# RG-LRU input product by seven products per pair of tiles, gates of a pair at 1024 columns

## The chip, the cores and the metric

The kernel runs on one core of one Trainium2 chip. The metric is the device time of one execution in microseconds (us); the median over several executions is compared. A profile of one execution gives, for each engine, every instruction with its start and duration.

The engines in this text: PE (TensorE) multiplies matrices into PSUM; ACT (ScalarE) applies functions and copies; DVE (VectorE) does elementwise work, scans and sums; POOL (GpSimd) does elementwise work too; SP issues most of the transfers (DMAs).

## The reference

Two layers on x of 1 x 1024 x 1024 (1024 tokens, 1024 channels), in float32. Layer 0: a retention and gated-delta mixer, then a convolution FFN. Layer 1: an RG-LRU mixer, then a convolution FFN. A norm closes it. The change lies in the mixer of layer 1:

```python
def rglru_mixer(hn, w_in, conv_w, conv_b, w_a, b_a, w_x, b_x, lam, w_out):
    gate, xr = jnp.split(hn @ w_in, 2, axis=-1)
    xr = causal_dwconv(xr, conv_w) + conv_b
    xb = xr.reshape(b, t, LRU_BLOCKS, LRU_BLOCK)
    r = sigmoid(einsum('btni,nij->btnj', xb, w_a) + b_a)
    i = sigmoid(einsum('btni,nij->btnj', xb, w_x) + b_x)
    log_a = -LRU_C * r * softplus(-lam)
    a = jnp.exp(log_a)
    u = jnp.sqrt(-jnp.expm1(2.0 * log_a)) * (i * xr)
    _, hs = lax.associative_scan(_linear_combine, (a, u), axis=1)
    y = gelu(gate) * hs
    return y @ w_out

h = h + rglru_mixer(rms_norm(h, norm_mix), ...)
h = h + conv_ffn(rms_norm(h, norm_ffn), w_up, conv_w, conv_b, w_down)
```

`hn @ w_in` is 1024 x 1024 by 1024 x 2048: 16 output tiles of 128 channels (8 gate tiles, 8 x tiles). The eight blocks of `w_a` and `w_x` are 128 x 128 each, so a tile's gates need that tile alone.

## The kernel before

Channels lie on the 128 partitions, tokens along the row: an activation tile is 128 x 1024, worked on as two halves of 512 columns (`HALF`). The residual is `self.H`, eight such tiles h0 to h7.

**Matmuls.** A float32 product is three matmuls (`mm3`, L313 to L315): weight hi by data hi, weight hi by data lo, weight lo by data hi. A matmul is 128 x 128 weights by 512 columns. Weights arrive from memory in `raw` buffers (seven) and are split by `split_quarter`: hi is a copy on ACT (L267), lo a subtraction on DVE (L268), in a ring of six pairs of buffers (`whi`, `wlo`).

**Pairs in seven products.** The FFN's up product takes two output tiles at once and halves all three dimensions: seven products in place of eight (`pair_products`). Each has 12 matmuls of 512 columns (four 128-row steps by three). The operands are seven combinations of blocks of the normed residual (`operand(o)`) and seven of the weights (`load_pair`; the sums are DVE operations at L288 to L290 and L303). Product o goes to the PSUM bank named by letter o of "ACACABA", so product 2 overwrites the bank of product 0. `pair_sums` empties the banks: products 0 to 2 are copied to `kept` tiles on ACT (L796), products 3 to 5 are added to a kept tile on DVE into the two `halo` tiles (L801), and product 6 is copied by ACT. `pair_halves` does the first pair of a stage on halves of 256 columns, while the second half of the operands is still being built.

**The stage before it.** The down product of layer 0's FFN (`ffn_d0`) runs all eight tiles for columns 0 to 511, then for columns 512 to 1023. Each finished tile half is added to h (L533). `down_x` then scales by the norm's gain and squares, for the norm over channels. Each tile half has 18 matmuls there. `lru_out`, the down product of the RG-LRU mixer, has 24 and ends with `down_pairs`, which also builds the seven operands of the pair scheme on DVE (L616, L626, L631) during its second half, applies the norm (`rtok`, a norm row on PE at L483) and hands over to `pair_halves`.

**RG-LRU mixer (`rglru`).** Sixteen plain products of 48 matmuls. The token norm R is applied when a product leaves PSUM. In step i: `proj_x(i)` (x tile), `stage_x(i)` (convolution: first tap on ACT L1051, three on DVE L1053; then split into hi and lo, L586 and L587), `stage_g(i-1)` (12 gate matmuls; tanh L1070 per half and gate; exp, tanh, sqrt at L1075, L1076, L1082 per half; DVE L1081, L1083, L1084 and scan L1085 per half), `stage_y(i-2)` (gate tile product, gelu L1095, product with the scan's result, stored to `y_dram`). So two products of 48 matmuls lie between the gates of one tile and those of the next. The y tiles come back as operands of `lru_out`.

**Order.** The scheduler orders DVE, ACT, POOL and SP by readiness estimates; every engine executes its queue strictly in order, so a waiting instruction holds up all behind it. PE's order is written by hand in the pair stages (`manual_schedule`).

## Time and profile before

| what | us |
|---|---|
| median of 3 executions | 2153.62 (2153.57 to 2155.07) |
| the profiled execution, its own time | 2152.99 |
| its span, first to last instruction | 2151.2 |
| PE, DVE, ACT, POOL busy | 2137.9, 1693.5, 1082.8, 98.2 |
| second half of `ffn_d0`, from | 1184 |
| RG-LRU products and gates | 1222 to 1416 |
| second half of `lru_out`, to | 1455 to 1497 |

Starts are counted from the first instruction. A busy time adds up the durations of an engine's instructions; a duration includes fill and drain, so back-to-back instructions overlap a little in the record and the start-to-start distance is what a queue full of them costs. The granted clock is 1.00 over the whole execution.

### The profile page before, as it was taken

Reading aid. Unit: us, or ns where it says so; the run is one execution under the profiler, and the core shown is the slowest. Engines: PE = TensorE matmul, PEld = TensorE weight load, DVE = VectorE, ACT = ScalarE, POOL = GpSimd, SP = SyncE. Lnnn points to the kernel's source line nnn. Section 1 sums busy time; section 2 is a strip of 40 time slices with the busy share of each in tenths; the row PEclk is TensorE's granted clock in tenths of the full one; section 3 lists DMA queues with packets and bytes.
Section 4 is the critical chain, followed back from the end, with each engine's and each line's share of the span. In section 5 each row is a group of like instructions: output and inputs, shape, how many; then the busy total and the mean of one; then the engine's idle time right before and its main releaser. Section 6 shows DMA issues by size and latency. Waiting matters only on the chain.

```text
span 2151.2 us, 29709 instructions
## 1 busy us (share of the span) xinstructions
PE 2137.9 (99%) x10716; PEld 1783.3 (83%) x10716; DVE 1693.5 (79%) x2565; ACT 1082.8 (50%) x1748; POOL 98.2 (5%) x114
## 2 busy tenths in 40 slices
PE   9999999999999999999999999999999999999998
PEld 7877889888888888888888888888888888888887
DVE  7995676656999889888866787778999889888645
ACT  6444433235665555555324476756655555554321
POOL 0102022300000000000000000000000000000001
PEclk9999999999999999999999999999999999999999
DMA  5354423444145445437636312242354345375542
GB/s 187 92 168 127 134 89 96 166 128 131 55 155 174 146 158 191 156 109 273 230 104 205 87 54 80 70 154 68 119 180 167 143 159 178 118 266 178 181 169 84
DMA packets 205171, 307.98 MB, mean 143 GB/s; under 512 B 29376, under 2 KB 92384, under 8 KB 205024
## 3 DMA queue, kind: packets, MB, share of 16 engines
q1 hardware_dynamic: 197760, 299.60, 41.9%
q10 hardware_dynamic: 6240, 5.97, 0.9%
q8 instruction: 84, 1.38, 0.3%
q0 software_dynamic: 1024, 0.53, 0.1%
q14 instruction: 63, 0.52, 0.1%
HBM read 215.27 MB, written 90.74 MB: 142 GB/s over the span
## 4 chain that ended last, share of the span: by engine, by line
PE 93%; DVE 3%; DMA 1%; issue 1%; SPq 0%; ACT 0%; POOL 0%; POOLq 0%; DVEq 0%; ACTq 0%
PE ps L313 28%; PE ps L314 28%; PE ps L315 28%; PE pc L313 1%; PE pc L314 1%; PE pc L315 1%; DVE l L1333 0%; DVE l L1331 0%; PE pc L483 0%; DMA l<-gc_dram 0%; DVE wlo L268 0%; PE ps L1508 0%; PE pc L1464 0%; PE ps L1606 0%; PE pc L1576 0%
## 5 line engine op out<-in xcount | busy, mean ns | idle before, releaser
L313 PE MATMUL ps<-s,whi 128*128 128x512 f32 (+1 forms) x2704 | 1054.5, 391 | 1.1 <-ACT s L383 0.7
L314 PE MATMUL ps<-s,whi 128*128 128x512 f32 (+1 forms) x2704 | 1047.9, 388 | 0.5 <-DVE s L900 0.5
L315 PE MATMUL ps<-s,wlo 128*128 128x512 f32 (+1 forms) x2704 | 1047.3, 388 | 0.0
L267 ACT CAST whi<-raw 128x512 fp32r<-128x512 f32 (+1 forms) x620 | 376.6, 613 | 628.4 <-PE ps L314 494.6
L313 PEld LDWEIGHTS ps<-s,whi 128*128 128x128 f32 x2704 | 507.8, 188 | 106.6 <-ACT s L383 1.3
L315 PEld LDWEIGHTS ps<-s,wlo 128*128 128x128 f32 x2704 | 507.7, 188 | 104.7 <-DVE wlo L268 0.6
L314 PEld LDWEIGHTS ps<-s,whi 128*128 128x128 f32 x2704 | 508.1, 188 | 102.5 <-DVE s L900 1.9
L268 DVE TENSOR_TENSOR wlo<-raw,whi 128x512 fp32r<-128x512 f32 (+1 forms) x620 | 415.7, 676 | 72.0 <-ACT whi L267 60.8
L828 DVE SCALAR_TENSOR_TENSOR t<-halo,cols,t 128x1024 f32<-128x1024 f32 x176 | 221.6, 1281 | 2.6 <-ACT t L826 1.6
L801 DVE TENSOR_TENSOR halo<-ps,kept 128x512 f32<-128x512 f32 (+1 forms) x138 | 91.8, 666 | 74.4 <-PE ps L315 73.2
L811 DVE TENSOR_TENSOR h<-ps,h 128x512 f32<-128x512 f32 x112 | 77.3, 690 | 78.8 <-PE ps L315 78.8
L826 ACT ACTIVATE t<-halo,cols 128x1024 f32<-128x1024 f32 x88 | 109.5, 1246 | 18.6 <-DVE halo L801 10.2
L796 ACT COPY kept<-ps 128x512 f32<-128x512 f32 (+1 forms) x138 | 77.1, 558 | 11.0 <-PE ps L315 9.5
L533 DVE TENSOR_TENSOR h<-ps,h 128x512 f32<-128x512 f32 (+1 forms) x72 | 45.2, 630 | 42.4 <-PE ps L315 42.3
L916 DVE TENSOR_TENSOR t<-t 128x1024 f32<-128x1024 f32 x44 | 53.6, 1219 | 0.0
L911 ACT ACTIVATE t<-t 128x1024 f32<-128x1024 f32 x44 | 46.7, 1062 | 10.5 <-DVE t L828 10.5
L852 ACT CAST t<-t 128x512 fp32r<-128x512 f32 x56 | 34.0, 621 | 35.3 <-DVE t L916 33.2
L401 ACT ACTIVATE t<-h 128x512 f32<-128x512 f32 (+1 forms) x49 | 27.3, 562 | 43.6 <-DVE h L533 43.6
L313 PE MATMUL ps<-s,s 128*128 128x256 f32 (+1 forms) x144 | 46.0, 320 | 0.0
L314 PE MATMUL ps<-s,s 128*128 128x256 f32 (+1 forms) x144 | 45.8, 318 | 0.0
L315 PE MATMUL ps<-s,s 128*128 128x256 f32 (+1 forms) x144 | 45.8, 318 | 0.0
L857 DVE TENSOR_TENSOR t<-t 128x512 f32<-128x512 f32 x64 | 43.9, 685 | 0.7 <-DMA sf_dram<-t 0.6
(339 smaller groups left out, 2124.5 us busy)
## 6 DMA issues: line engine op xcount, KB each, us to landing
raw<-in_ffn_up_dram SPq DMA_DIRECT2D x176, 256.0 KB, 2.7
s<-pf_dram SPq DMA_DIRECT2D x112, 256.0 KB, 5.3
sf_dram<-t SPq DMA_DIRECT2D x72, 256.0 KB, 2.5
raw<-in_ffn_w_dram SPq DMA_DIRECT2D x64, 256.0 KB, 2.9
t<-sf_dram SPq DMA_DIRECT2D x58, 256.0 KB, 4.5
pf_dram<-t SPq DMA_DIRECT2D x56, 256.0 KB, 2.6
pf_dram<-lo SPq DMA_DIRECT2D x56, 256.0 KB, 2.5
raw<-in_mix_in_dram SPq DMA_DIRECT2D x52, 256.0 KB, 2.9
```

Of the source, the lines that this page charges most:

```text
L267: self.nc.scalar.copy(hi[:, 0:w], raw[:, 0:w])
L268: eng.tensor_tensor(lo[:, 0:w], raw[:, 0:w], f32(hi[:, 0:w]), ALU.subtract)
L313: mm(ps, whi, xhi, start=start, stop=False)
L314: mm(ps, whi, xlo, start=False, stop=False)
L315: mm(ps, wlo, xhi, start=False, stop=stop)
L796: A.copy(kept[o], ps)
L801: V.tensor_tensor(dst(i, j), v(ps), v(kept[k]), ALU.add)
L811: V.tensor_tensor(h(*to[o]), ps.rearrange("p (h c) -> p h c", c=256), h(*to[o]), ALU.add)
L826: A.activation(t, buf[:, 2:2 + T], AF.Identity, scale=w(0), bias=self.col(f"ffn_cb{layer}", tile_i))
L828: V.scalar_tensor_tensor(t, buf[:, 2 + j:2 + j + T], w(j), t, ALU.mult, ALU.add)
L911: A.activation(tg, tg, AF.Silu)
L916: V.tensor_tensor(tg, tg, tv, ALU.mult)
```

## The change

The 16 input products become eight pairs in seven products (`lru_p`: an x pair, then the gate pair of the same two tiles, four times). The end of `ffn_d0` therefore builds the seven operands, as `lru_out`'s end does, and `down_x` goes. Each half of h is stored to `h_dram` on the way, since the residual's tiles h0 to h7 now serve as buffers of the mixer; they are loaded again ahead of `lru_out`. The gates of the even tile of a pair come after product 5 of the gate pair, those of the odd tile after product 6 (`then`); the rest of the gate work (`stage_h`) is done for both tiles together and 1024 columns at a time, after the last gate. To POOL go the weights' lo parts from the second gate pair to the last (`lo_engine`), the first convolution tap of the odd tiles, and the last product of `stage_y` for three of the four pairs. The small columns (`few`) with the softplus of `lru_lam` move to the kernel's start.

By instruction counts over the kernel: matmuls of 512 columns 8472 before and 8292 now, of 256 columns 624 and 792; POOL elementwise operations of 512 columns 28 and 69, of 1024 columns none and 10, of 256 columns none and 5.

```diff
             if layer == 1:
-                for i in range(8):
-                    o.append((("lru_in", 8 + i), 2))
-                    if i >= 1:
-                        o.append((("lru_g", i - 1), 1))
-                    if i >= 2:
-                        o.append((("lru_in", i - 2), 2))
-                o += [(("lru_g", 7), 1), (("lru_in", 6), 2), (("lru_in", 7), 2)]
+                for t in range(4):
+                    o.append((("lru_p", 2 * t), 7))
+                    o += [(("lru_p", 2 * t + 1), range(6)), (("lru_g", 2 * t), 1)]
+                    o += [(("lru_p", 2 * t + 1), range(6, 7)), (("lru_g", 2 * t + 1), 1)]
                 o += out("lru_out", 0) + out("lru_out", 1)
...
+    def rows(self, key):
+
+        src = self.I["lru_in" if key[0] == "lru_p" else key[0]]
+        if key[0].startswith("ffn_up"):
+            return src[key[1]], src[NPAIR + key[1]]
+        if key[0].startswith("ffn_w"):
+            c, t = key[1:]
+            return src[c, 2 * t], src[c, 2 * t + 1]
+        t, gate = divmod(key[1], 2)
+        first = 2 * t + (0 if gate else 8)
+        return src[first], src[first + 1]
...
-        s = lambda raw: self.split_quarter(raw, V, place=self.extra.pop(len(self.loaded), None))
+        s = lambda raw: self.split_quarter(raw, self.lo_engine, place=self.extra.pop(len(self.loaded), None))
...
-    def down_x(self, ys, name, gain):
+    def down_pairs(self, ys, name, gain, groups=None, keep=None):
 
         def then(n, st, m, h):
-            st["whole"] = True
-            self.square_step(st, m, self.norm_step(st, m, gain, n))
-            if m == KT - 1:
-                if n == 0:
-                    self.norm_beside(st, n)
-                else:
-                    self.steps(8, self.norm_rest(st, n, 3))
-        self.down_norm(ys, name, gain, lambda n: self.groups(1), then)
-
-    def down_pairs(self, ys, name, gain):
-
-        def then(n, st, m, h):
+            if keep is not None:
+                self.nc.sync.dma_start(keep[m][:, n * HALF:(n + 1) * HALF], h)
             st["bufs"] = [self.halo[n][:, 4 + HALF:]] + [b[:, 4:4 + HALF] for b in self.halo]
             st["whole"] = n == 0
             self.square_step(st, m, h)
...
                 if m == 5:
                     self.late = self.late_operands(st, gain)
                 self.late["scale"](m)
-        self.down_norm(ys, name, gain, self.groups, then)
+        self.down_norm(ys, name, gain, groups or self.groups, then)
...
-    def pair_products(self, layer, p, then=None):
-
-        key = (f"ffn_up{layer}", p)
+    def pair_products(self, key, then=None):
...
-            self.down_x(last, f"ffn_d{layer}", gain)
+            self.h_dram = self.tc.dram_tile([KT, P, T], F32, name="h_dram")
+            self.down_pairs(last, f"ffn_d{layer}", gain, lambda n: self.groups(1), self.h_dram)
...
+            if i % 2:
+                nc.gpsimd.tensor_scalar(x, buf[:, 1:1 + T], w(0), self.col("lru_cb", i), ALU.mult, ALU.add)
+            else:
+                A.activation(x, buf[:, 1:1 + T], AF.Identity, scale=w(0), bias=self.col("lru_cb", i))
             for j in (1, 2, 3):
                 V.scalar_tensor_tensor(x, buf[:, 1 + j:1 + j + T], w(j), x, ALU.mult, ALU.add)
-            xh, xl = (xs[:, (2 * (i % 2) + j) * T:(2 * (i % 2) + j + 1) * T] for j in range(2))
+            xh, xl = (self.h_tile(2 * (i % 2) + j, F32R) for j in range(2))
...
-                    A.activation(t, ps, AF.Tanh, scale=0.5, bias=b[:, i:i + 1])
-                    th[n, q] = t
-            for n in range(2):
-                a = u()
-                A.activation(a, th[n, 0], AF.Exp, scale=spm4[:, i:i + 1], bias=spm4[:, i:i + 1])
-                A.activation(th[n, 0], th[n, 0], AF.Tanh, scale=sp2[:, i:i + 1], bias=sp2[:, i:i + 1])
-                th[n, 2] = a
-            for n in range(2):
-                sl = slice(n * HALF, (n + 1) * HALF)
-                sq, tx, a = th[n, 0], th[n, 1], th[n, 2]
-                V.scalar_tensor_tensor(tx, tx, 1.0, x[:, sl], ALU.add, ALU.mult)
-                A.activation(sq, sq, AF.Sqrt)
+                    A.activation(H[2 * (i % 2) + q][:, sl], ps, AF.Tanh, scale=0.5, bias=b[:, i:i + 1])
+        def stage_h(t):
+            decay = [self.h_tile(m) for m in range(2)]
+            two = [(i, H[2 * (i % 2)], H[2 * (i % 2) + 1], decay[i % 2], xr[i][0]) for i in (2 * t, 2 * t + 1)]
+            for i, th, tx, a, x in two:
+                A.activation(a, th, AF.Exp, scale=spm4[:, i:i + 1], bias=spm4[:, i:i + 1])
+                A.activation(th, th, AF.Tanh, scale=sp2[:, i:i + 1], bias=sp2[:, i:i + 1])
+                V.scalar_tensor_tensor(tx, tx, 1.0, x, ALU.add, ALU.mult)
+            for i, sq, tx, a, x in two:
+                A.activation(sq, sq, AF.Sqrt, scale=0.25)
                 V.scalar_tensor_tensor(sq, a, 1.0, sq, ALU.add, ALU.mult)
-                V.scalar_tensor_tensor(tx, tx, 0.5, sq, ALU.mult, ALU.mult)
-                V.tensor_tensor_scan(hs[:, sl], a, tx, 0.0 if n == 0 else hs[:, HALF - 1:HALF], ALU.mult, ALU.add)
-            st[i] = hs
-        def stage_y(i):
-            hs = st.pop(i)
-            unit = self.unit("lru_in", i)
-            def evac(n, sl, ps):
-                g = u() if i < 6 else self.halo[i % 2][:, 4 + sl.start:4 + sl.stop]
-                V.tensor_tensor(g, ps, self.R[:, sl], ALU.mult)
-                A.activation(g, g, AF.Gelu_apprx_tanh)
-                V.tensor_tensor(hs[:, sl], g, hs[:, sl], ALU.mult)
-            self.project(unit, evac)
-            if i < 6:
-                nc.sync.dma_start(self.y_dram[i], hs)
-            return hs
-        proj_x(0)
-        for step in range(8):
-            if step == 0:
-                proj_x(1)
-            elif step > 1:
-                proj_x(step)
-            stage_x(step)
-            if step >= 1:
-                stage_g(step - 1)
-            if step >= 2:
-                stage_y(step - 2)
-        stage_g(7)
-        stack.close()
-        self.open_s2(self.ctx)
-        ys = [self.load_split(self.y_dram[i], self.place2(i)) for i in range(4)]
-        hs = [stage_y(6), stage_y(7)]
-        ys += [self.load_split(self.y_dram[4 + i], self.place1(i)) for i in range(2)]
-        ys += [self.split(hs[i], self.place1(2 + i)) for i in range(2)]
-        self.down_pairs(ys, "lru_out", gain)
+                V.tensor_tensor(tx, tx, sq, ALU.mult)
+                V.tensor_tensor_scan(x, a, tx, 0.0, ALU.mult, ALU.add)
+        def stage_y(t):
+            for i in (2 * t, 2 * t + 1):
+                g = gs[i] = self.R if i % 2 == 0 else f32(self.parts.tile([P, T], F32R, tag="lo", name="lo"))
+                A.activation(g, self.halo[i % 2][:, 4:4 + T], AF.Gelu_apprx_tanh)
+            stage_h(t)
+            for i in (2 * t, 2 * t + 1):
+                (V if t == 3 else nc.gpsimd).tensor_tensor(gs[i], gs[i], xr.pop(i)[0], ALU.mult)
+                if i < 6:
+                    nc.sync.dma_start(self.y_dram[i], gs[i])
+        ys = {}
+        def load_y(*ks):
+            for k in ks:
+                ys[k] = self.load_split(self.y_dram[k], self.place2(k))
+        def then(t, o):
+            if o >= 5:
+                stage_g(2 * t + o - 5)
+            if t == 3 and o in (1, 2, 4):
+                load_y(*{1: (0, 1), 2: (2, 3), 4: (4, 5)}[o])
+        pair = lambda s: ("lru_p", s)
+        with self.tc.manual_schedule(engines={mybir.EngineType.PE}):
+            second = self.pair_products(pair(1), partial(then, 0))
+            self.pair_halves(pair(0), pair(1), second)
+            self.lo_engine = nc.gpsimd
+            stage_x(0)
+            stage_x(1)
+            self.run(second)
+        for t in range(4):
+            if t:
+                self.run(self.pair_products(pair(2 * t)))
+                stage_x(2 * t)
+                stage_x(2 * t + 1)
+                if t == 3:
+                    self.lo_engine = V
+                self.run(self.pair_products(pair(2 * t + 1), partial(then, t)))
+            stage_y(t)
+        H = self.H = [self.h_tile(m) for m in range(KT)]
+        for m in range(4):
+            nc.sync.dma_start(H[m], self.h_dram[m])
+        for i in (6, 7):
+            ys[i] = self.split(gs[i], self.place1(i - 6))
+        self.after(26, lambda: [nc.sync.dma_start(H[m], self.h_dram[m]) for m in range(4, KT)])
+        self.down_pairs([ys[i] for i in range(KT)], "lru_out", gain)
```

**ACT between two steps.** Of before, the row of ACT around one tile's gates (names: `us` small gate tiles, `whi` weight parts, `pc` the PSUM tile of the gate matmuls):

```order
L1070 ACTIVATE us<-pc,ba 128x512
L1051 ACTIVATE t<-halo_99,cols 128x1024
L1070 ACTIVATE us<-pc,bx 128x512
L1070 ACTIVATE us<-pc,ba 128x512
L1070 ACTIVATE us<-pc,bx 128x512
L1075 ACT_TABLE_LOAD
L1075 ACTIVATE us<-us,spm_10748 128x512 x2
L1076 ACTIVATE us<-us,sp_10746 128x512
L586 CAST xs<-t 128x1024
L1076 ACTIVATE us<-us,sp_10746 128x512
L1082 ACT_TABLE_LOAD
L1082 ACTIVATE us<-us 128x512 x2
```

Of the change, ACT from the second tile's last tanh to the first copies of the next pair (`h_...` are the reused residual tiles, `R` and `lo` the gelu tiles, `kept<-ps` the copy that empties product 0's bank):

```order
L1047 ACTIVATE h_10743<-pc,few 128x512
L1065 ACTIVATE lo<-halo_99 128x1024
L1053 ACT_TABLE_LOAD
L1053 ACTIVATE h_11639<-h_10740,few 128x1024
L1053 ACTIVATE h_11640<-h_10742,few 128x1024
L1054 ACTIVATE h_10740<-h_10740,few 128x1024
L1054 ACTIVATE h_10742<-h_10742,few 128x1024
L1057 ACT_TABLE_LOAD
L1057 ACTIVATE h_10740<-h_10740 128x1024
L1057 ACTIVATE h_10742<-h_10742 128x1024
L269 CAST whi<-raw 128x512
L786 COPY kept<-ps 128x512
```

The chain of one tile has become a chain of two tiles at twice the width, and the copy of product 0 of the next pair stands behind all of it. The product that overwrites that bank, product 2, waits on PE for this copy.

**DVE at the same place**, of the change, from the gate chain to the sums of the next pair (`L1058` to `L1060` need the sqrt above; `raw<-raw` are weight sums; `halo<-ps,kept` the sums of products 3 to 5):

```order
L293 TENSOR_TENSOR raw<-raw 128x512
L1055 SCALAR_TENSOR_TENSOR h_10743<-h_10743,t 128x1024
L1058 SCALAR_TENSOR_TENSOR h_10740<-h_11639,h_10740 128x1024
L1058 SCALAR_TENSOR_TENSOR h_10742<-h_11640,h_10742 128x1024
L1059 TENSOR_TENSOR h_10741<-h_10741,h_10740 128x1024
L1059 TENSOR_TENSOR h_10743<-h_10743,h_10742 128x1024
L1060 SCALAR_TENSOR_TENSOR t<-h_11639,h_10741 128x1024
L1060 SCALAR_TENSOR_TENSOR t<-h_11640,h_10743 128x1024
L292 TENSOR_TENSOR raw<-raw 128x512
L306 TENSOR_TENSOR raw<-raw 128x512
L791 TENSOR_TENSOR halo_98<-ps,kept 128x2x256
L791 TENSOR_TENSOR halo_99<-ps,kept 128x2x256
```

The weight sum at `L306` needs a `raw` buffer that a weight lo on POOL reads. The sums of the next pair's products stand behind the scans. On POOL the rows at this place are:

```order
L270 TENSOR_TENSOR wlo<-raw,whi 128x256
L270 TENSOR_TENSOR wlo<-raw,whi 128x512
L270 TENSOR_TENSOR wlo<-raw,whi 128x256
L270 TENSOR_TENSOR wlo<-raw,whi 128x512 x8
L1068 TENSOR_TENSOR R<-R,t 128x1024
L270 TENSOR_TENSOR wlo<-raw,whi 128x512
L1068 TENSOR_TENSOR lo<-lo,t 128x1024
```

**DVE near the end of `ffn_d0`.** Of before, from one addition to h (L533) to the next but one (`s_96` takes the scaled tiles, `t<-t` sums squares):

```order
L533 TENSOR_TENSOR h_89<-ps,h_89 128x512
L268 TENSOR_TENSOR wlo<-raw,whi 128x256
L384 SCALAR_TENSOR_TENSOR s_96<-h_89,cols,s_96 128x512
L405 TENSOR_TENSOR t<-t 128x512
L268 TENSOR_TENSOR wlo<-raw,whi 128x512
L533 TENSOR_TENSOR h_90<-ps,h_90 128x512
L268 TENSOR_TENSOR wlo<-raw,whi 128x256
L384 SCALAR_TENSOR_TENSOR s_96<-h_90,cols,s_96 128x512
L405 TENSOR_TENSOR t<-t 128x512
L268 TENSOR_TENSOR wlo<-raw,whi 128x512
L533 TENSOR_TENSOR h_91<-ps,h_91 128x512
```

Of the change, at the same place, from one addition to h (L536) to the next (`t<-t,pc` scales by the norm, `s_4166<-t,s_4166` and the `t<-t` of 1024 columns build operands):

```order
L536 TENSOR_TENSOR h_89<-ps,h_89 128x512
L624 TENSOR_TENSOR t<-t 128x1024
L408 TENSOR_TENSOR halo_99<-halo_99 128x512
L270 TENSOR_TENSOR wlo<-raw,whi 128x256
L619 TENSOR_TENSOR t<-t,pc 128x1024
L609 TENSOR_TENSOR s_4166<-t,s_4166 128x1024
L270 TENSOR_TENSOR wlo<-raw,whi 128x512
L624 TENSOR_TENSOR t<-t 128x1024
L536 TENSOR_TENSOR h_90<-ps,h_90 128x512
```

Between two additions there were four operations of at most 512 columns; here there are seven, four of them 1024 columns wide.

More of the change, by code (lines that the diff above doesn't have):

```diff
@@ L129, in __init__ @@
         pad(self.perm, 49, "pad1")
-        self.H = [self.perm.tile([P, T], F32, name=f"h{m}") for m in range(KT)]
+        self.H = [self.h_tile(m) for m in range(KT)]
         self.s1 = self.perm.tile([P, 2, 32, 256], F32R, name="s1")
@@ L211, in quarter_order @@
                 o += [x for _ in range(2) for x in out("ffn_d0", 1)]
-        return [(key, j) for key, n in o for j in range(n)]
+        return [(key, j) for key, n in o for j in (range(n) if isinstance(n, int) else n)]
     @staticmethod
@@ L233, in unit @@
         return [self.quarter(key, j, hold) for j in range(2)]
[L235 to L251 removed]
+    def rows(self, key):
[8 more added lines that the diff above has]
+        return src[first], src[first + 1]
+    def load_all(self):
+        pair = None
+        for key, j in self.order[len(self.loaded):]:
+            if key[0].startswith(("ffn_up", "ffn_w", "lru_p")):
+                if j == 0:
+                    pair = self.pairs.pop(key, None) or self.load_pair(key)
+                yield next(pair)
+                continue
+            src = self.I[key[0]]
             for i in key[1:]:
                 src = src[i]
[L254 to L259 removed]
+            c, w = j * HALF, min(HALF, src.shape[1])
+            w = min(w, src.shape[1] - c)
+            raw = self.raw()
+            self.nc.sync.dma_start(raw[:, 0:w], src[:, c:c + w])
+            yield self.split_quarter(raw, self.lo_engine, w)
     def raw(self):
@@ L722, in pair_halves @@
         self.prefetch(first)
-        up = self.I[key[0]]
         self.eager = True
-        pair = self.pairs[key[0], p + 1] = self.load_pair(up[p + 1], up[NPAIR + p + 1])
+        pair = self.pairs[after] = self.load_pair(after)
         next(pair)
@@ L932, in ffn @@
         with self.tc.manual_schedule(engines={mybir.EngineType.PE}):
-            second = self.pair_products(layer, 1, partial(after, 1))
-            self.pair_halves(layer, 0, second)
+            up = lambda p: (f"ffn_up{layer}", p)
+            second = self.pair_products(up(1), partial(after, 1))
+            self.pair_halves(up(0), up(1), second)
             after(0, 5)
@@ L939, in ffn @@
         for p in range(2, NPAIR):
-            self.run(self.pair_products(layer, p, partial(after, p)))
+            self.run(self.pair_products(up(p), partial(after, p)))
             if p < NPAIR - 1:
@@ L1024, in rglru, with sm @@
+        used = [0]
+        def sm(name):
+            used[0] += 8
+            return self.few[:, used[0] - 8:used[0]]
+        sp, sp2, spm4, nl, ba, bx = (sm(n) for n in ("sp", "sp2", "spm4", "nl", "ba", "bx"))
         V.tensor_scalar(nl, self.cols_of("lru_lam"), -1.0, None, ALU.mult)
         self.softplus(sp, nl, sm, "l")
-        sp2 = sm("sp2")
         V.tensor_scalar(sp2, sp, 2.0, None, ALU.mult)
-        spm4 = sm("spm4")
         V.tensor_scalar(spm4, sp, -4.0, None, ALU.mult)
-        ba, bx = sm("ba"), sm("bx")
@@ L1058, in stage_g @@
         def stage_g(i):
-            x, xh, xl = xr.pop(i)
-            hi, lo = self.quarter(("lru_g", i))
-            hs = self.t()
-            th = {}
+            x, xh, xl = xr[i]
+            hi, lo = self.quarter(("lru_g", i), 0, self.hold)
             for n in range(2):
```

60 lines of the change are left out of this document (11 added, 49 removed).

## Prediction

> **What bounds the kernel now.** I read the page first: busy shares, granted clock, chain of waits.
>
> ```profile
> PE 2137.9 (99%) x10716; PEld 1783.3 (83%) x10716; DVE 1693.5 (79%) x2565; ACT 1082.8 (50%) x1748; POOL 98.2 (5%) x114
> PEclk9999999999999999999999999999999999999999
> PE 93%; DVE 3%; DMA 1%; issue 1%; SPq 0%; ACT 0%; POOL 0%; POOLq 0%; DVEq 0%; ACTq 0%
> ```
>
> PE is the bound from end to end, at full clock. Fewer matmuls are worth their whole time, as long as nobody makes PE wait. Then the stages that the change touches, in windows (columns: length; busy us of PE, PEld, DVE, ACT, POOL; clock; DMA share; GB/s):
>
> ```profile
> 1184.00:1217.00 33.00, 33.00 (x154) 26.92 (x152) 24.52 (x50) 19.03 (x32) 2.00 (x5) 1.00 0.40 115
> 1222.00:1392.00 170.00, 170.00 (x752) 140.75 (x751) 125.76 (x163) 116.17 (x158) 0.00 (x0) 1.00 0.21 66
> 1455.00:1497.00 42.00, 42.00 (x197) 34.85 (x190) 38.87 (x52) 27.01 (x49) 1.01 (x1) 1.00 0.24 73
> ```
>
> In the RG-LRU stage (1222 to 1392) PE never waits, with DVE at 74% and ACT at 68% beside it. In the second half of ffn_d0 (1184 on) DVE fills 24.5 of 33 us. In that of lru_out, which also builds pair operands, it fills 38.9 of 42: nearly all. What PE pays per matmul is the distance between starts, in PE's timeline:
>
> ```profile
> 1299.82 0.39 PE L314 MATMUL ps<-s,whi 128*128 128x512 f32 x1
> ...
> 1300.73 0.39 PE L315 MATMUL ps<-s,wlo 128*128 128x512 f32 x1
> ...
> 1503.05 0.28 PE L313 MATMUL ps<-s,whi 128*128 128x256 f32 x1
> ...
> 1503.89 0.28 PE L314 MATMUL ps<-s,whi 128*128 128x256 f32 x1
> ```
>
> Four steps of 512 columns take 0.91, so 0.2267 each; seven of 256 take 0.84, so 0.12 each.
>
> **The gain.** The counts give 180 matmuls of 512 columns fewer and 168 of 256 more: 180 x 0.2267 = 40.8, less 168 x 0.12 = 20.2, is 20.6. The norm sums and row in the middle of the halves cost about 1.1 (one such row below). Net gain 19.5 us. Everything else in the sum is a new wait of PE.
>
> **A, the end of ffn_d0.** DVE now does lru_out's work there, but a tile half has 18 matmuls in place of 24. The additions to h, first and last of the second half, in DVE's timeline, and PE's norm row after lru_out:
>
> ```profile
> 1183.27 0.68 DVE L533 TENSOR_TENSOR h<-ps,h 128x512 f32<-128x512 f32 x1
> ...
> 1211.24 0.69 DVE L533 TENSOR_TENSOR h<-ps,h 128x512 f32<-128x512 f32 x1 [0.68 <-PE ps L315]
> ...
> 1497.15 0.69 DVE L533 TENSOR_TENSOR h<-ps,h 128x512 f32<-128x512 f32 x1
> ...
> 1499.61 0.17 DVE L465 TENSOR_SCALAR rtok<-halo 128x4 f32<-128x4 f32 x1
> 1500.98 1.16 PE L483 MATMUL pc<-ident,rtok 128*128 128x128 f32 x8 [0.25 <-POOL rtok L466]
> ```
>
> The window is 1211.24 - 1183.27 = 28.0 us. Between the same two additions the changed DVE row holds 15 operations of 1024 columns, 24 of 512 and 5 of 256 (order of instructions). Durations and overlap come from these groups and this place of DVE's timeline:
>
> ```profile
> L268 DVE TENSOR_TENSOR wlo<-raw,whi 128x512 fp32r<-128x512 f32 x64 | 42.7, 685 | 15.7 <-ACT whi L267 15.6
> L1053 DVE SCALAR_TENSOR_TENSOR t<-halo,cols,t 128x1024 f32<-128x1024 f32 x24 | 30.8, 1281 | 9.6 <-ACT t L1051 9.5
> L1085 DVE TENSOR_TENSOR_SCAN t<-us 128x512 f32<-128x512 f32 x8 | 9.8, 1219 | 0.0
> L587 DVE TENSOR_TENSOR xs<-t,xs 128x1024 fp32r<-128x1024 f32 x8 | 9.7, 1219 | 0.5 <-ACT xs L586 0.5
> L268 DVE TENSOR_TENSOR wlo<-raw,whi 128x256 fp32r<-128x256 f32 x7 | 2.9, 417 | 0.0
> ...
> 263.58 0.68 DVE L1461 TENSOR_TENSOR kept<-pc,l 128x512 f32<-128x512 f32 x1
> 264.19 0.67 DVE L1465 TENSOR_TENSOR kept<-kept,pc 128x512 f32<-128x512 f32 x1
> ```
>
> A queue's distance is about 0.07 less than the duration: 0.61 for 512 columns, 1.14 for 1024, 0.35 for 256. 15 x 1.14 + 24 x 0.61 + 5 x 0.35 = 33.5, against 28.0: the last addition comes 5.5 late. Behind it seven more of 512 columns stand ahead of rtok: 0.69 + 7 x 0.61 + 0.3 = 5.2, against 1499.61 - 1497.15 = 2.46 in lru_out. PE there waited 0.25 at the norm row with all else equal. A = 5.5 + 2.7 + 0.25 = 8.5. Ends: 5 (the seven are done while PE and ACT make the sums), 11 (the first half leaves DVE a backlog of 2.5).
>
> **B, the first x pair.** Its gates need tile 0's convolution and split, and the halves have drawn part of the gate pair's products ahead, so PE has little between. DVE owes both tiles' six taps, 6 x 1.21 = 7.3, and the even tile's split 1.14. I take 4.5; ends 1 (the taps run in between sums) and 6. The odd tile's tap on POOL has no row for its form; the nearest lie between one of POOL's 512-column operations below (1.28) and two (2.56), and it runs beside the even tile's taps.
>
> **C, the three boundaries between steps.** After the last gate matmul PE has products 0 and 1 of the next x pair, 24 x 0.2267 = 5.44 us (17 matmuls, 3.85, at the first boundary). Product 2 overwrites product 0's bank and so waits for ACT's copy, which ACT's row puts behind the whole gate chain. The chain at 512 columns, in ACT's timeline, and groups that give its length at 1024:
>
> ```profile
> 1389.09 0.67 ACT L1070 ACTIVATE us<-pc,bx 128x512 f32<-128x512 f32 x1
> 1389.78 1.28 ACT L1075 ACT_TABLE_LOAD   x1
> 1391.08 1.52 ACT L1075 ACTIVATE us<-us,spm 128x512 f32<-128x512 f32 x2
> 1392.51 1.51 ACT L1076 ACTIVATE us<-us,sp 128x512 f32<-128x512 f32 x2
> 1394.03 1.28 ACT L1082 ACT_TABLE_LOAD   x1
> 1395.33 1.15 ACT L1082 ACTIVATE us<-us 128x512 f32<-128x512 f32 x2
> 1396.50 1.28 ACT L1095 ACT_TABLE_LOAD   x1
> ...
> L1051 ACT ACTIVATE t<-halo,cols 128x1024 f32<-128x1024 f32 x8 | 9.9, 1235 | 0.6 <-DVE halo L373 0.6
> L1075 ACT ACTIVATE us<-us,spm 128x512 f32<-128x512 f32 x16 | 12.2, 812 | 0.1
> L267 ACT CAST whi<-raw 128x512 fp32r<-128x512 f32 x49 | 29.3, 616 | 37.8 <-PE ps L314 33.9 <-ACT t L608 2.3 <-DMA raw<-in_lru_outa_dram 1.6
> L796 ACT COPY kept<-ps 128x512 f32<-128x512 f32 (+1 forms) x138 | 77.1, 558 | 11.0 <-PE ps L315 9.5
> ```
>
> Six activations with two table loads take 1396.50 - 1389.78 = 6.72 us. Twice the width adds 1235 - 812 = 423 ns each: 6.72 + 6 x 0.42 = 9.3. From the last gate matmul: 0.2 to start, last tanh 0.69, one gelu of 1024 about 1.0, chain 9.3, a weight hi 0.5, the copy 0.56: 12.2. PE waits 12.2 - 5.44 = 6.8, twice, and 12.2 - 3.85 = 8.4 once: C1 = 22. Ends 19 and 24 (one weight hi more or less, a gelu already done).
>
> Behind it comes DVE. Its two STTs, two products, two scans of 1024 columns (about 2.25 each, twice L1085) and two weight sums, 2.4 + 2.3 + 4.5 + 1.2 = 10.4, start at about 11.3 and end at 21.7. The sum of product 4, which product 6 needs, follows; PE by then has ended product 5 at about 22.9. Undisturbed, DVE is just in time. But POOL now works at the same place, and the two engines hold each other up in this trace (DVE's and POOL's timelines, one behind the other):
>
> ```profile
> 261.83 1.28 POOL L1541 TENSOR_TENSOR t<-t,l 128x512 f32<-128x512 f32 x1 [38.55 <-DMA g_dram<-t]
> 263.19 1.62 POOL L1580 TENSOR_TENSOR l<-t,l 128x512 f32<-128x512 f32 x1
> 277.57 1.29 POOL L1541 TENSOR_TENSOR t<-t,l 128x512 f32<-128x512 f32 x1 [6.71 <-DVE l L1540]
> ...
> 262.75 0.92 DVE L268 TENSOR_TENSOR wlo<-raw,whi 128x512 fp32r<-128x512 f32 x1 [1.05 <-PE pc L1460]
> 278.07 1.33 DVE L1452 TENSOR_TENSOR kept<-kept,l 128x512 f32<-128x512 f32 x1
> ```
>
> The DVE subtraction from 262.75 lasts 0.92 in place of 0.685 and ends 0.56 after POOL's end at 263.11; the product from 278.07 lasts 1.33 and ends 0.54 after POOL's at 278.86. Both look as if they stood still until POOL was through. With four POOL weights (1.15 left of each) and one product of 1024 (2.3) taking turns with DVE's chain, DVE ends at 21.7 + 6.9 = 28.6, and PE waits up to 5.7 more at each boundary. Ends of C2: 0 and 18; I take 4 each, 12, nearer the upper end since both rows show the full stand.
>
> [...]
>
> **D, the tail.** After the last gates nothing is left but lru_out, which has 61 matmuls, 13.8 us, before it needs y tile 6. From the last gate matmul: 0.2, tanh 0.69, a table load 1.28, two gelus 2.0, chain 9.3: 13.5. The first sqrt ends 0.6 before that, and DVE runs STTs, products, scans and the last multiplication from 12.9: 2.4 + 2.3 + 4.5 + 1.1 = 10.3, so R's y tile is there at 23.2; cast and split 0.6 each and queue distances bring 24.5 to 25.3. D = 11 (10 to 13).
>
> **Sum.** 2152.99 - 19.5 + 8.5 + 4.5 + 22 + 12 + 11 = 2191.5. The profiled run lies 0.6 below the median of the three, so nothing is added. Costed at nothing: the 16 stores and 8 loads of h and the 6 y tiles, 256 KB halves on SP's queue, which the windows show loaded at 0.21 to 0.40; and the softplus at the start, a few operations of 8 columns (each under 0.2 like L465 above). If SP's queue were late with weights instead, PE would show waits for DMA, some us per pair.
>
> **Rivals.**
> - *POOL and DVE do not get in each other's way here*: C2 is 0 and B about 2. For: DVE has a quarter of idle time in the stage of before. Against: the two rows. 2191.5 - 12 - 2.5 = 2177.
> - *The clock falls in the waits.* The warm-up at the start, PE's timeline:
>
> ```profile
> 1.16 4.15 PE L1624 MATMUL pc<-t 128*128 128x128 f32 x20 [1.16 <-POOL l L1627]
> ```
>
>   20 matmuls of 128 columns in 4.15 us, 0.21 each, where eight of the same size took 1.16 at the norm row, 0.145 each with fill: PE out of idleness ran at about half of what it does later. If each of the six waits of over 4 us brought back one such stretch, at 2 us lost each, 12 us come on top: 2203. Against: before has no wait of that length, so nothing shows it. [...]
> - *The other side: PE does not wait for ACT's copy.* If ACT reaches product 0's copy within the 5.44 us of products 0 and 1, C and most of D go: A 5, B 1, D 11 - 6.8 = 4 remain, 10 in all, against 19.5 gained: 2143.5. The point is 5.4 us from the last gate matmul to the copy, against 12.2 worked out; half of that chain would have to be done before the last gate, and it needs the last tanh. Together the waits must stay under 19.5 us for this kernel to be faster.
>
> **How the numbers follow.** The sum as worked out (within 10 us of 2191.5) 0.45; no contention, 2177, 0.22; clock, 2203 (with upper ends up to 2220), 0.23; the other side, 2143.5, 0.07; about equal 0.03. The lower ends of all terms, 5 + 1 + 19 + 0 + 10 = 35 less 19.5, give 2168.5; a boundary wait half as long as I make it gives 2160. The upper ends, 11 + 6 + 24 + 18 + 13 = 72, give 2205.5, and with the clock 2218. So 2160 to 2218. A measurement of this kernel can tell about 0.2%, 4.3 us, from no change: faster 0.07, same 0.03, slower 0.90.
>
> **What would show it.** In the changed profile: PE idle of 5 to 11 us at the end of ffn_d0, released by POOL's or DVE's rtok; three idle stretches of 6 to 9 us released by the ACT copy of product 0 (or by the weight hi ahead of it), each 17 to 24 matmuls behind the last gate; a second, shorter one in the same pair released by a DVE sum; one of about 11 us ahead of lru_out's second half, released by DVE. The DVE operations of 1024 columns beside POOL work would last longer than 1.28, and POOL's weight lo longer than 1.28. The clock row would show less than 9 in slices 22 to 28 if the second rival holds. I am wrong if PE is as full as before in these stages, or if its waits have DMA as the releaser.

## The result, and the profile after

The change takes 2229.88 us (median of four executions, 2226.89 to 2231.84) against 2153.6: a ratio of 1.0352, 95% interval 1.0334 to 1.037. The sign of the forecast was right, its size was not: 2191.5 was forecast, and 2218 was the end of its range. The profiled execution took 2231.84, its span is 2230.1 (before 2152.99 and 2151.2). The kernel before, timed again beside each group of experiments below, had medians of 2153.47 to 2154.2, so their times can be compared. One execution of the last kernel below (the tail in order) took 4339.42 us and is left out of its median.

The page of the change, busy shares and the clock row:

```profile
PE 2149.0 (96%) x10728; PEld 1786.8 (80%) x10728; DVE 1736.7 (78%) x2536; ACT 1105.7 (50%) x1793; POOL 198.1 (9%) x166
PEclk9999999999999999999999988889999999999999
```

PE is no longer full, and four slices of the clock row, those of the mixer, show an 8; the mean granted clock is 0.981, against 0.999 before, where it falls only in the last 6.4 us (0.50 there). What PE waited for between 1180 and 1520 us, in the view of waits (columns: us in total, times, longest):

```profile
PE ps L316 <- ACT whi L269: 26.3, 4, 9.1
PE ps L316 <- DVE halo L791: 17.0, 4, 5.6
PE ps L316 <- ACT s L579: 6.4, 1, 6.4
PE pc L316 <- ACT h L579: 3.1, 1, 3.1
PE pc L477 <- ACT halo L404: 2.9, 1, 2.9
PE pc L477 <- DVE halo L408: 2.4, 1, 2.4
PE ps L316 <- ACT kept L786: 1.9, 2, 1.0
PE pc L486 <- POOL rtok L469: 1.8, 1, 1.8
```

First row: the three waits at product 2 (9.1 the longest) and one of 2.9 at the tail. Second: the three waits for the sum of product 4, and one of 1.6 ahead of lru_out. Third: the y tile at the tail. Fourth: the first x pair. The rows for L477 and L486 are the norm at the end of ffn_d0, and `kept` is two short waits for copies. The chain ahead of product 2, in ACT's timeline:

```profile
1286.88 1.28 ACT L1053 ACT_TABLE_LOAD   x1
1288.18 2.37 ACT L1053 ACTIVATE h<-h,few 128x1024 f32<-128x1024 f32 x2
1290.45 2.36 ACT L1054 ACTIVATE h<-h,few 128x1024 f32<-128x1024 f32 x2
1292.83 1.28 ACT L1057 ACT_TABLE_LOAD   x1
1294.13 2.00 ACT L1057 ACTIVATE h<-h 128x1024 f32<-128x1024 f32 x2
1296.04 0.60 ACT L269 CAST whi<-raw 128x512 fp32r<-128x512 f32 x1
1296.55 0.58 ACT L786 COPY kept<-ps 128x512 f32<-128x512 f32 x1
```

ACT never pauses. From the first table load to the end of the sqrts it takes 9.2 us (9.3 forecast); weight hi and copy stand behind, the copy from 1296.55, though product 0's last matmul started at 1284.48. Then PE and its clock, in PE's timeline of the same place:

```profile
1287.21 0.39 PE L318 MATMUL ps<-s,wlo 128*128 128x512 f32 x1
1296.69 1.28 PE L316 MATMUL ps<-s,whi 128*128 128x512 f32 x2 [9.10 <-ACT whi L269]
1297.77 0.63 PE L317 MATMUL ps<-s,whi 128*128 128x512 f32 x1
1298.19 0.63 PE L318 MATMUL ps<-s,wlo 128*128 128x512 f32 x1
...
1302.72 0.40 PE L317 MATMUL ps<-s,whi 128*128 128x512 f32 x1
1302.95 0.39 PE L318 MATMUL ps<-s,wlo 128*128 128x512 f32 x1
```

Behind the wait, matmuls start 0.43 us apart in place of 0.23, for some 5 us; the granted clock from 1280 to 1303 us is 0.78. So the second rival held as well as the forecast.

A ledger follows from the distances between starts of PE's matmuls: what exceeds 0.2267 or 0.12 is a wait where the distance is more than 2.4 times that, else slow clock. Stages are cut at the additions to h. A wait by these distances is some 0.15 us longer than in the view of waits.

| part | forecast | in the profiled execution |
|---|---|---|
| fewer matmuls, net | -19.5 | -18.5 |
| A, end of ffn_d0 | 8.5 | 7.6 |
| B, first x pair | 4.5 | 3.2 |
| C1, product 2 | 22 | 23.8 |
| C2, product 6 | 12 | 15.9 |
| D, tail | 11 | 10.8 |
| waits under 2 us elsewhere | 0 | 8.9 |
| low clock behind waits | 0 (12 in the rival) | 19.5 |
| start of the kernel | 0 | 7.8 |
| sum | 38.5 | 79 |

The last row is the difference of the spans, 78.9.

### The profile page after: what moved, and what is told of

Its sections match the earlier page's. It is cut to its first block, busy times and chain, and to the rows that moved or that the text cites. A ratio compares the mean times of both kernels' runs of the same rounds, so it can differ in the third digit from the quotient of the medians.

```text
span 2230.1 us, 29926 instructions
## 1 busy us (share of the span) xinstructions
PE 2149.0 (96%) x10728; PEld 1786.8 (80%) x10728; DVE 1736.7 (78%) x2536; ACT 1105.7 (50%) x1793; POOL 198.1 (9%) x166
## 3 DMA queue, kind: packets, MB, share of 16 engines
q0 software_dynamic: 1024, 0.53, 0.1%
## 5 line engine op out<-in xcount | busy, mean ns | idle before, releaser
L269 ACT CAST whi<-raw 128x512 fp32r<-128x512 f32 (+1 forms) x643 | 390.4, 613 | 651.1 <-PE ps L317 483.1
L270 DVE TENSOR_TENSOR wlo<-raw,whi 128x512 fp32r<-128x512 f32 (+1 forms) x597 | 401.2, 678 | 65.9 <-ACT whi L269 54.9
L818 DVE SCALAR_TENSOR_TENSOR t<-halo,cols,t 128x1024 f32<-128x1024 f32 x176 | 221.5, 1280 | 2.1 <-ACT t L816 1.0
L791 DVE TENSOR_TENSOR halo<-ps,kept 128x512 f32<-128x512 f32 (+1 forms) x165 | 108.2, 658 | 79.4 <-PE ps L318 78.4
L786 ACT COPY kept<-ps 128x512 f32<-128x512 f32 (+1 forms) x165 | 91.4, 554 | 16.3 <-PE ps L318 14.1
L469 POOL TENSOR_TENSOR rtok<-rtok,npow 128x4 f32<-128x4 f32 (+1 forms) x10 | 9.9, 993 | 960.6 <-PE ps L316 608.6
L270 POOL TENSOR_TENSOR wlo<-raw,whi 128x512 fp32r<-128x512 f32 (+1 forms) x46 | 74.0, 1622 | 80.3 <-ACT whi L269 77.2
L536 DVE TENSOR_TENSOR h<-ps,h 128x512 f32<-128x512 f32 (+1 forms) x72 | 45.1, 629 | 38.7 <-PE ps L318 38.6
L306 DVE TENSOR_TENSOR raw<-raw 128x512 f32<-128x512 f32 x68 | 53.1, 781 | 8.0 <-POOL wlo L270 7.4
L605 ACT CAST s<-t 128x1024 fp32r<-128x1024 f32 x39 | 40.9, 1050 | 34.3 <-DVE t L677 18.8
L291 DVE TENSOR_TENSOR raw<-raw 128x512 f32<-128x512 f32 x68 | 46.9, 689 | 13.1 <-POOL wlo L270 11.2
L292 DVE TENSOR_TENSOR raw<-raw 128x512 f32<-128x512 f32 x68 | 53.0, 780 | 0.5
```

What stands on the lines that cost most here:

```text
L269: self.nc.scalar.copy(hi[:, 0:w], raw[:, 0:w])
L270: eng.tensor_tensor(lo[:, 0:w], raw[:, 0:w], f32(hi[:, 0:w]), ALU.subtract)
L306: V.tensor_tensor(sum1, a12, sum2, ALU.subtract)
L786: A.copy(kept[o], ps)
L791: V.tensor_tensor(dst(i, j), v(ps), v(kept[k]), ALU.add)
L818: V.scalar_tensor_tensor(t, buf[:, 2 + j:2 + j + T], w(j), t, ALU.mult, ALU.add)
```

## The experiments

Each kernel is the change with one or more edits; `...` marks where a cut leaves lines out.

**Softplus late.** The first operation of the softplus reads a finished residual tile, so it can't run at the start:

```diff
+        last = self.H[3]
...
-        V.tensor_scalar(nl, self.cols_of("lru_lam"), -1.0, None, ALU.mult)
+        V.scalar_tensor_tensor(nl, last[:, 0:8], 0.0, self.cols_of("lru_lam"), ALU.mult, ALU.subtract)
```

> The small operations of the softplus wait for a residual tile of the first half of ffn_d0 and so leave the kernel's start; nothing else is moved by hand. Theory (queue at the start): 7.8 us of the 79 that the change lost lie ahead of the first addition to h (497.2 before, 505.0 in the change), because DVE's row put work ahead of rtok; the first addition comes back to 497 to 499, the time falls by 6 to 8 us to about 2222. Rival (the start is slower because of the buffers or transfers of the change): first addition stays at 505, time 2230.

2224.57 us; the first addition to h comes at 497.1, where the change has 505.0. DVE and PE at the start, of the change (rtok, then PE's matmuls that wait):

```profile
28.52 0.16 DVE L468 TENSOR_SCALAR rtok<-t 128x4 f32<-128x4 f32 x1
...
26.06 1.92 PE L1206 MATMUL ps<-h,l 128*32 128x512 f32 x16 [1.64 <-DVE l L1663]
30.32 0.38 PE L486 MATMUL pc<-ident,rtok 128*128 128x128 f32 x1 [2.34 <-POOL rtok L469]
```

and of this kernel:

```profile
20.24 0.17 DVE L468 TENSOR_SCALAR rtok<-t 128x4 f32<-128x4 f32 x1
...
23.33 1.05 PE L486 MATMUL pc<-ident,rtok 128*128 128x128 f32 x8
```

The small operations themselves are short, as priced (0.16 us for one of 8 columns at 28.59 of the change). But the scheduler built another order of DVE around them, in which rtok stands behind twelve more operations of 512 columns, and PE waits for it. The theory holds: the first addition to h comes 7.9 us earlier, which is the whole of the ledger's last row. The medians differ by 5.3 us, the profiled spans by 7.5 (2222.6); the change's four executions lie 5 us apart, and its profiled one is the longest.

**Copies ahead of the chain.** The gelus, products 0 to 2 of the next x pair with their copies, then the gate chain:

```diff
...
+            for _ in range(3):
+                if following:
+                    next(following)
             stage_h(t)
...
```

> Products 0 to 2 of the next x pair and their copies stand ahead of the gate chain on ACT (behind the two gelus). Theory (ACT's queue order makes the three long waits): the three waits of 9.3, 7.3 and 7.3 us at product 2 go, and with them 6.5 us at the low clock behind them; the waits at product 6 (5.0, 5.8, 5.0) stay or change by a few us, since the scans now stand between the sums: about 2200 (2190 to 2210). Rival (DVE and POOL are the bound, PE would wait as long at a sum): the waits at product 6 grow to 10 or more each, time 2222 to 2232.

2222.64 us, in the rival's range. The long waits at product 2 went, and others came. What PE waits for in the mixer here:

```profile
PE pc L316 <- ACT h L579: 10.8, 3, 5.4
PE pc L316 <- DVE halo L791: 6.7, 2, 5.9
PE ps L316 <- ACT whi L269: 4.8, 2, 3.0
```

The largest is the split of the next x tile ahead of its gates: a convolution tap on DVE took 1.85 us on average (43.3 us for 24) against 1.28 in before. So ACT's order made the three waits, and behind them DVE and POOL were the bound as well.

**Weight lo parts on DVE.** `self.lo_engine = V` from the start to the end of the mixer.

> All weight lo parts stay on DVE; POOL keeps the taps and the last products. Theory (DVE and POOL exclude each other): a lo costs DVE 0.61 itself but stood in its way for up to 1.15 on POOL, so DVE's 1024-column operations in the mixer return to 1.2 to 1.3 us, and the waits at product 6 fall from 15.9 to about 6 in sum, with 4 less at the low clock: about 2216. Rival (no exclusion, POOL only takes work off DVE): DVE has 25 us more to do, the waits at product 6 grow to 23, time 2237 or more.

2221.34 us, 8.5 below the change; the waits at product 6 fell only from 15.9 to 13.9, where the theory had 6. Its other half held: DVE's products of 1024 columns took 1.22 us again (second group of rows below).

**No POOL work.** In addition the last products on DVE and the odd tiles' first tap on ACT.

> As e3_lo_on_dve, and the last products on DVE, the odd tiles' first tap on ACT: no POOL work in the mixer. [...] Rival (POOL takes work off at no cost): 7 us slower than e3_lo_on_dve.

2203.11 us, 18 below the one before, where a difference of at most 4 was expected. The groups show why: of the change (POOL and DVE), of weight lo on DVE (POOL and DVE), and of no POOL (DVE):

```profile
L270 POOL TENSOR_TENSOR wlo<-raw,whi 128x512 fp32r<-128x512 f32 x41 | 67.9, 1669 | 73.7 <-ACT whi L269 70.7 <-PE pc L317 2.9
L1068 POOL TENSOR_TENSOR R<-R,t 128x1024 f32<-128x1024 f32 x3 | 12.9, 4297 | 6.7 <-PE ps L318 4.5 <-DVE t L1060 2.2
L1059 DVE TENSOR_TENSOR h<-h,h 128x1024 f32<-128x1024 f32 x6 | 13.6, 2305 | 0.0
```

```profile
L1068 POOL TENSOR_TENSOR R<-R,t 128x1024 f32<-128x1024 f32 x3 | 12.7, 4230 | 117.6 <-DVE t L1060 117.6
L270 DVE TENSOR_TENSOR wlo<-raw,whi 128x512 fp32r<-128x512 f32 x48 | 44.9, 955 | 8.9 <-ACT whi L269 8.9
L1059 DVE TENSOR_TENSOR h<-h,h 128x1024 f32<-128x1024 f32 x8 | 9.4, 1218 | 0.0
```

```profile
L270 DVE TENSOR_TENSOR wlo<-raw,whi 128x512 fp32r<-128x512 f32 x56 | 36.9, 682 | 6.6 <-ACT whi L269 6.4
L1059 DVE TENSOR_TENSOR h<-h,h 128x1024 f32<-128x1024 f32 x8 | 9.5, 1218 | 0.0
```

DVE's product of 1024 columns takes 2.3 us beside POOL's weight lo parts and 1.22 without; with the lo parts on DVE, these stretch in turn (955 against 682 ns) beside POOL's last products, of which the first takes 4.2. So the count of DVE's operations is not what costs: DVE does more of them here and the kernel is faster. In this order of removal the last products and taps gave more (18) than the weight lo parts (8.5). Not all of it need be the two engines holding each other up. In the change DVE also stood still for results of POOL between 1262 and 1480 us:

```profile
DVE raw L291 <- POOL wlo L270: 11.2, 3, 4.0
DVE t L1033 <- POOL t L1029: 8.8, 4, 3.6
DVE raw L306 <- POOL wlo L270: 7.4, 6, 1.8
```

With the weight lo parts on DVE 3.1 us of this are left, without POOL none. So in the step from the second kernel to the third the stretched operations are the larger part (48 weight lo parts at 955 in place of 682 ns are 13 us); in the step before it the two effects aren't separated. In the kernel without POOL the waits for DVE's sums in the mixer are small:

```profile
PE ps L316 <- ACT whi L269: 24.0, 3, 9.8
PE ps L316 <- DVE halo L791: 2.8, 3, 1.1
```

C1 is untouched, C2 is down to 2.8.

**Less DVE work at the end of ffn_d0.** For the second half's weights:

```diff
+            if seen.get(key, 0) == 2:
+                hi = self.wsp.tile([P, HALF], F32R, tag="whi", name="whi")
+                self.nc.scalar.copy(hi[:, 0:w], raw[:, 0:w])
+                yield hi, hi
...
```

> The lo parts of the down product's weights in the second half of ffn_d0 are not computed (the hi part is read in their place), which takes 7 subtractions of 512 columns and 5 of 256, about 6 us, off DVE between the additions to h; the result is not the reference's there. Theory (DVE's queue is 5.5 us too long for the 28 us of matmuls): the last addition comes 28 to 29 us after the first (35.0 in the change), PE's waits at the norm sums and the norm row, 7.7 us, fall to 2 or less, with 2 at the low clock: time 2220 to 2222. Rival (PE waits there for the squares on ACT or for POOL's power, not for DVE's queue): waits of 6 us or more remain, time 2228.

2226.2 us, 3.7 below the change, which is within the spread of the executions (2223.93 and 2228.48 here), so only the trace tells. The additions to h of the change stand here:

```profile
1191.05 0.69 DVE L536 TENSOR_TENSOR h<-ps,h 128x512 f32<-128x512 f32 x1 [0.59 <-PE ps L318]
...
1225.97 0.69 DVE L536 TENSOR_TENSOR h<-ps,h 128x512 f32<-128x512 f32 x1
```

34.9 us apart, where DVE's queue was worked out as 33.5. With the subtractions left out, and with them the lo parts of these weights, it is 31.2, not 28 to 29, and PE's waits at the norm are 2.3 and 2.2 in place of 7.1 in sum. The direction is that of the theory, the size falls between theory and rival: DVE had 1.8 us to wait for the norm row of the first half, and after that its queue was still full to the last addition. That more work off DVE would end the rest wasn't tried.

**Filling the waits, first form.**

```diff
...
+            if key[0] == "lru_p" and key[1] in (2, 4, 6) and o in (2, 6):
+                ps, x = self.pc(), self.operand(o - 1)
+                for k in range(24 if o == 2 else 20):
+                    self.nc.tensor.matmul(ps, last[0][:, 0:P], x[:, :, k % 8, :], start=True, stop=True, skip_group_check=True)
...
```

> Matmuls that nothing reads fill most of the waits ahead of product 2 (24 of 512 columns, 5.4 us) and product 6 (20, 4.5 us) of the x pairs; all else is the change. Theory (the clock falls because PE stands still): the stretches at half clock behind these six waits, 12 us of excess in sum, go, the waits become shorter by what is filled, and the time falls by 8 to 12 us to about 2219. Rival (the clock falls for another reason, such as load): the stretches stay, and the time is 2230 or more.

2242.55 us, 12.7 slower than the change: above the rival's 2230, but not for the rival's reason. The filler read a weight buffer of the ring and took a bank; waits of 3 to 4 us were left or came anew (the longest 4.0), and the mean granted clock was 0.988 and 0.989, against 0.999 before. This form tells nothing about the clock.

**Second form.** 28 matmuls ahead of product 2 alone, weights and data from the operands, into the bank that product 5 takes later.

> As e6_filler, but its 28 matmuls (6.3 us) stand only ahead of product 2, read the operands of product 0 as weights too, so that they hold no weight buffer, and write the bank that product 5 takes later. ACT's row is that of the change. Theory (the clock falls because PE stands still for 3 us or more): the three long waits shrink to about 3, 1 and 1 us at the same end, the 6.5 us of excess at half clock behind them go, those behind the waits at product 6 stay: 2223 to 2226 against the change's 2229.9. Rival (the clock falls for another reason): the stretches stay behind product 2, 2229 or more.

2229.36 us, ratio 1.0352 (1.0335 to 1.0369). There is no gain against the change, and the number is the rival's, but the trace agrees with the theory. The three waits at product 2, 9.3, 7.3 and 7.3 in the change, became 3.3, 0.95 and 0.95 (by the distances); behind the two short ones no slow stretch is left (granted clock 1.00 from 1345 to 1370 and from 1410 to 1430 us, where the change has 0.82 and 0.73 in windows of 19 us at the same waits), behind the 3.3 there is one (0.91 from 1280 to 1300). And the waits for the sum at product 6 grew from 5.0, 5.8, 5.1 to 5.3, 6.9, 6.9. Of this kernel, the view of waits:

```profile
PE ps L316 <- DVE halo L796: 19.1, 4, 6.8
PE ps L316 <- ACT whi L269: 7.6, 4, 3.1
```

So at product 2 the slow stretches went where the waits fell from 7.3 to 0.95 us, and a slow stretch ahead of another wait cost nothing here: PE only comes earlier to a sum that DVE ends when it did (counted from the last gate matmul, within 0.9 us of the change in all three steps). The 19.5 us of the ledger are not what a steady clock would give back; only the stretches with no wait behind them count.

**No POOL, softplus late, copies ahead.**

> e4_no_pool with e1_softplus_late and e2_copies_ahead together. If the three act on different waits: e4's 2203.1 less 7.3 (start) less its waits at product 2 (24.5) with 4.8 at the low clock is 2166.5, plus waits at sums of a few us each where scans now stand between: 2165 to 2178. If the copies' place only helped because POOL stretched everything, 2190 or more.

2185.63 us: better than each, but 8 to 21 us above what the theory expected, and under the rival's 2190. In the mixer (1257 to 1400 us) PE now waits for weight lo parts, which stand in DVE's queue:

```profile
PE ps L318 <- DVE wlo L270: 9.0, 2, 5.1
PE ps L316 <- ACT kept L786: 2.5, 4, 1.5
```

**The same, with less DVE work in the mixer.** The input product's weights have no lo part (hi is read twice), so the result misses what these would add.

> e7_no_pool_ahead with the lo parts of the input product's weights not computed (hi read in their place; the result is not the reference's), 13 to 14 subtractions, some 8 us of DVE, fewer per step. If what is left of waits in the mixer of e7_no_pool_ahead (about 21 us with the clock) is DVE being full, they fall to 6 or less: 2165 to 2172. If it is the gate chain on ACT, 2180 or more.

2168.85 us, and the same view of the same stretch:

```profile
PE ps L322 <- ACT kept L792: 2.7, 5, 0.7
PE pc L322 <- DVE halo L797: 1.4, 2, 1.2
```

Without some 8 us of DVE work a step the mixer runs nearly at PE's pace (PE is busy 49.3 of 52 us and 42.1 of 44 in two steps, at a granted clock of 1.00), so what is left of C without POOL stands in DVE's queue. Whether the queue is too full or in the wrong order is not shown: this edit also removes the very operations that PE waited for, and in the kernel with those waits DVE is busy 41.7 of 52 us and 36.3 of 44 in the two steps. (One wait of 5.6 us at the last x pair stays.)

**One tile's chain at a time.** The even tile's chain directly behind its gates, the odd tile's behind two copies of the next pair.

> No POOL work, softplus late, and the gate chain for one tile at a time: the even tile's right after its gates, the odd tile's behind two copies of the next pair. Against e7_no_pool_ahead (2185.6): DVE's chain is split in two pieces between which sums pass, but ACT has two more table loads a step and the odd tile's tanh stands behind the even tile's chain. If DVE's long uninterrupted chain makes e7's waits for weight lo (5.1 and 3.9 us), these go: 2175 to 2182. If ACT's chain still decides (16 to 17 us from the even tile's last gate to the copy, against 10.9 of matmuls): three waits of 5 to 6 at product 2, 2185 to 2195. The tail is shorter in both, by about 6.

2191.87 us, as its second case said for ACT's chain, though not by a wait at product 2: at each boundary PE waits 3.9 to 4.2 us for ACT's tanh, and at two of the three, ahead of it, 2.2 for ACT's copy of product 6:

```profile
PE ps L316 <- ACT h L1048: 12.0, 3, 4.2
```

Shorter chains didn't help while the next pair's work stood behind them on ACT, which by the expectation also has two more table loads a step (1.28 us each in the change).

**The tail in halves.** Of the last step's gate chain, columns 0 to 511 first:

```diff
+            for n in range(2):
+                c = slice(n * HALF, (n + 1) * HALF)
+                ...
+                    self.split_half(gs[i][:, c], self.place1(i - 6)[n])
```

> e7_no_pool_ahead with the last step's gate chain in halves of 512 columns, the first half's y tiles split before the second half's chain ends, as lru_out's first pass reads columns 0 to 511 only. Theory (D is the length of the chain at 1024 columns): the waits of 10.8 us ahead of lru_out fall to about 5, the time is 5 to 8 below e7_no_pool_ahead. Rival (D is the wait for the transfers of the earlier y tiles or of h): same time as e7_no_pool_ahead.

2186.34 us, nothing gained. ACT's timeline shows the first half's casts (L579 at 1447.80) behind the second half's exp and tanh:

```profile
1442.94 1.28 ACT L1069 ACT_TABLE_LOAD   x1
1444.23 1.52 ACT L1069 ACTIVATE h<-h,few 128x512 f32<-128x512 f32 x2
1445.66 1.51 ACT L1070 ACTIVATE h<-h,few 128x512 f32<-128x512 f32 x2
1447.80 0.62 ACT L579 CAST s<-R 128x512 fp32r<-128x512 f32 x1 [0.63 <-DVE R L1077]
```

PE still waits 6.3 us for them. (This kernel also kept two products of 1024 columns on DVE at its end, which nothing reads.) So the order was fixed by hand:

> e7_no_pool_ahead with the last step's gelus and gate chain in halves, as in e8_tail_halves, but ACT and DVE keep the order written: the casts of the first half's y tiles stand ahead of the second half's chain, and no product of 1024 columns is left behind. Theory (D is the chain's length; e8 gained nothing because ACT's row put the casts behind the second half's exp and tanh): gates to first cast 12 to 13 us against 13.8 us of matmuls, the waits of 10.7 us ahead of lru_out fall to 4 or less, and with the clock behind them the time is 2174 to 2179 against e7's 2185.6. Rival (the wait is for the weights of lru_out or the loads of the earlier y tiles): waits of 8 or more remain, 2184 or more.

2179.54 us, 6 below e7_no_pool_ahead and 0.5 above the theory's range. PE's waits ahead of lru_out between 1430 and 1480 us, there and here:

```profile
PE ps L316 <- ACT s L579: 6.4, 1, 6.4
PE ps L316 <- ACT whi L269: 2.8, 1, 2.8
```

```profile
PE ps L316 <- ACT s L579: 1.6, 2, 1.1
```

D is the chain's length. Some of it comes back at lru_out's norm (waits of 2.7 and 1.6 us that e7 hadn't); that this is so because the second half's chain now falls nearer to it was not tested.

No version beats the kernel before: the best that computes all takes 2179.54 (ratio 1.0117, 1.0097 to 1.0137).

## Why the prediction was wrong

- **The gain.** 19.5 forecast, 18.5 found. Right.
- **A, B, C1, C2, D.** 58 forecast; 61.3 found, each within 4 us of its term. The chain on ACT (9.3 forecast, 9.2 found) and DVE's queue in ffn_d0 (33.5 and 1.5 of waiting against 34.9) were read rightly from durations of before. The order of the queues, with these durations, gave the waits. For D the chain was right, but 3 of its 10.8 us are a wait for a weight hi on ACT, which the forecast hadn't. For B, PE waited for the split's cast on ACT, which stands behind DVE's taps (six of them take 9.9 us from 1261.32).
- **POOL and DVE.** C2 was put between its ends at 12 and came out at 15.9; experiments e3 and e4 put the work on POOL at 26.8 us of time in all (2229.88 to 2203.11), more than C2's upper end of 18: it also stretched the taps (1.56 us on average, 1.28 in before) ahead of B and what followed in each step (scans 2.82 on average, 2.28 in e4_no_pool), and the low clock behind the waits that went is in it. One reading made the term small: 1.28 was near the shortest (1.27) of the group of POOL's products of 512 columns in before that it came from, whose mean was 1.50; the weight lo parts took 1.67.
- **The clock.** The step that failed: "Against: before has no wait of that length, so nothing shows it." The clock was made a rival with a chance of 0.23 and left out of the sum. In the trace of the change it fell behind every wait of over 3.3 us, and the slow matmuls behind waits come to 19.5 us, the largest term that the sum lacked. The price was mis-sized too: 2 us for each of six waits, 12, where the ledger has 19.5. It was no rival at all, but a surcharge on the forecast's own mechanism. 2191.5 + 12 would have been 2203.5. The 19.5 is what the ledger holds, not what a steady clock would save: the second filler took away two of the three stretches behind product 2 and the time stayed, since the waits at product 6 grew. How much of the rest is a loss of its own no run shows.
- **The start.** The other step that failed: the softplus was costed at nothing, as "a few operations of 8 columns". Its durations were right and its cover was not: 7.8 us. The trace shows the small operations among the squares, with rtok twelve large operations later than before; the forecast didn't look at the order there.
- **Small waits.** 8.9 us of waits under 2 us had no term: three of 1.0 to 1.8 us make up 4 (two for ACT's copies, one for DVE's sum), the rest are under 1 us each. No experiment tests them.
- **The range.** The upper end added 12 for the clock to the upper ends of the terms. With the start's 7.8 and the small waits it would have held the time.

## What to carry to other kernels

When a forecast creates waits of several us on PE, the low clock behind them belongs in the same sum, not in a rival, as far as no later wait takes it up (here 19.5 us, behind waits of up to 9.3). A copy that frees a PSUM bank should not stand behind a long chain on the same queue (here 9.2 us of chain, and waits of 23.8 in three steps); but moving it pays only as far as the next engine has room, and here DVE hadn't (2229.88 to 2222.64 us). At the end of a stage, where nothing covers it, the length of a merged, wider chain is paid for in waits (10.8 us here). An operation without inputs to wait for can be scheduled anywhere: look at what it is put ahead of, not at how long it takes (7.8 us here, for operations such as the one of 0.16).
